# Both seven-product phases of a transformer layer in a written order of all engines, with other chunks in the first down projection

## The chip, the cores and the metric

The kernel runs on one core of a Trainium2 chip. A core has TensorE (PE, matmuls into eight PSUM banks), VectorE (DVE), ScalarE (ACT), GpSimd (POOL), SyncE (SP, which issues the transfers here) and 16 DMA engines. The metric is the time on the device of one execution, in microseconds (us), as the median of several runs. The profiled execution is a further one, and has its own time.

## The reference

One layer over 512 latent tokens and 256 context tokens, of width 1024, in float32. What matters here are its two feed-forward layers, FFN1 on all 768 tokens and FFN2 on the 512 latent ones:

```python
def swiglu(h, w1, w3, w2):
    return (jax.nn.silu(h @ w1) * (h @ w3)) @ w2

def ffn_sublayer(h_in, shift, scale, gate, norm_w, w1, w3, w2):
    h = modulate(rms_norm(h_in, norm_w), shift, scale)
    return h_in + 0.5 * gate * swiglu(h, w1, w3, w2)
...
    mx = jnp.split((jax.nn.silu(c) @ w_ada + b_ada)[:, None, :], N_MOD, axis=-1)
    x = ffn_sublayer(x, mx[0], mx[1], mx[2], norm1_w, ffn1_w1, ffn1_w3, ffn1_w2)
    ...
    x = ffn_sublayer(x, mx[6], mx[7], mx[8], norm3_w, ffn2_w1, ffn2_w3, ffn2_w2)
```

Between them lie attention and a gated MLP over chunks ("the middle" below). `w1` and `w3` are 1024 by 2816 each, `w2` is 2816 by 1024. The vectors `mx` and `mc` (shift, scale and gate) come from a product of `w_ada` (1024 by 9216) with one vector for each kind of token.

## The kernel before

**Numbers.** A float32 operand is split into a rounded high part and a remainder: a cast on ACT (L103) and a subtraction on VectorE (L104), both into buffers of `Stream` with five slots (`OPS`). `mm3` (L128) multiplies with three matmuls: high by high (L131), high by low (L132), low by high (L133).

**Up projection.** The 2816 columns are 22 tiles of 128, numbered f. For f = 0 and 1 they are computed while the modulation vectors arrive, for f = 2 and 3 plainly (`up1`), and from f = 4 on by `Winograd` (L593): one f with both weights is a 2 by 2 block problem, solved with seven products instead of eight. Each product (`prod`, L588) is four k-tiles of `mm3`, so 12 matmuls, of 384 columns in FFN1 and 256 in FFN2. The tokens' sums (B11, T1 and so on) are made once ahead of the phase. The weights' sums are made for each unit f from a 1 MB block (two `block` buffers): an addition (L607) and three subtractions (L629 to L631), on GpSimd; for FFN2's first unit they are on VectorE. So a unit needs seven operands of 128 by 512, each split by ACT and VectorE.

A unit has four accumulators X, Y, Z, W. In `head` it is product B11 into X, copied to p1. In `mid` T1 goes into Z, B21 into X (then silu into sl), T2 into Y (then u2 = Y + p1, L636) and T3 into W (then u3 = W + u2 and u3 = Z + u3, L638 and L639). In `tail` T4 is added into W (then times sl, and split into the tile g: L649, L650 and `g_split`, L325) and B22 into Z (then silu, times u3, and split). For even f the accumulators are four single banks `mm`; for odd f they are two tiles `big` of two banks each, with X and Z in one and Y and W in the other. `run` (L660) traces `head` of f + 1 between `mid` and `tail` of f.

**Down projection.** After some units a chunk of n tiles g is multiplied with its rows of `w2` (`down`): for each of eight output tiles and each column group (two of 384 in FFN1, one of 512 in FFN2) one `mm` bank gets 3n matmuls and is added into x by VectorE (L340 in FFN1, with an instruction of 256 columns for the latent and one of 128 for the context tokens of a group; L346 in FFN2). Its weights come in 512 KB pieces into three `raw` buffers. FFN1's chunks are 3, 3, 4, 4, 3, 5 and FFN2's 4, 4, 4, 4, 2, 4. FFN1's last chunk runs with the normalisation of the middle.

**The modulation vectors.** From f = 2 on, 80 dots (L234, one `w_ada` piece of 128 by 1024 with the vector, on VectorE, its piece in a `raw` buffer) are traced in small steps: eight behind f = 2 and f = 3 each, then four to a unit.

**What sets the order.** A tile scheduler orders the instructions of each engine by its own estimate of time, starting from the traced program; only what is traced through `Pinned` (L49) or `keep_in_program_order` keeps the written order. Before, both seven-product phases and their downs are left to the scheduler. The start, and the stretch ahead of FFN2's units (with `nc.ordered` set), are pinned on VectorE, ACT and GpSimd.

Of the kernel before, what the change touches and what calls it, by code (L numbers as in the profile page):

```python
# [8 lines left out]
F32 = mybir.dt.float32  # L9
# [7 lines left out]
P = 128  # L17
D = 1024
NK = D // P
# [7 lines left out]
SCALE = QH ** -0.5  # L27
CHUNKS1 = [3, 3, 4, 4, 3, 5]
CHUNKS2 = [4, 4, 4, 4, 2, 4]
# [30 lines left out]
class Core:  # L60


    def __init__(self, tc):
        self.nc, self.ordered = tc.nc, False
        self.pinned = {e: Pinned(tc, getattr(tc.nc, e)) for e in ("vector", "scalar", "gpsimd")}

    def __getattr__(self, name):
        return self.pinned[name] if self.ordered and name in self.pinned else getattr(self.nc, name)


class Halves:
# [65 lines left out]
def layer_kernel(ctx: ExitStack, tc: tile.TileContext, xT, wfirst, wst, wada, wuq, wkpe, cols, wrope, vnw, rope, out):  # L137
# [8 lines left out]
    ps = ctx.enter_context(tc.tile_pool(name="ps", bufs=1, space=PSUM))  # L146

    def big():
        return ps.tile([P, 2, 512], F32, tag="big", bufs=2, name=f"big_{nc.next_id()}")
# [374 lines left out]
    def g_tile(f):  # L524
        pool, bufs = (gp, 3) if f % 5 < 3 else (gp2, 2)
        gt[f] = tuple(pool.tile([P, 768], F32R, tag=t, bufs=bufs, name=f"{t}_{nc.next_id()}") for t in ("gh", "gl"))
        return gt[f]
# [28 lines left out]
    def down(f0, n, u0, groups, evac, dts=range(NK), cache=None):  # L556
        us = {} if cache is None else cache
        for dt in dts:
            for g, gn in groups:
# [9 lines left out]
                evac(pt, dt, g, gn)  # L569

    starts1 = [sum(CHUNKS1[:i]) for i in range(len(CHUNKS1))]
    starts2 = [sum(CHUNKS2[:i]) for i in range(len(CHUNKS2))]
# [19 lines left out]
    class Winograd:  # L592
# [16 lines left out]

        def head(self, f):  # L610
            n = self.n
            if self.ready[0] != f:
                self.prep(f)
            q, s1, eng = self.ready[1:]
            a11 = st.operand(q[0])
            bigs4 = bigs(4) if f % 2 else None
            mms = None if f % 2 else [mm() for _ in range(4)]
            banks = [bigs4[i] for i in (0, 2, 1, 3)] if f % 2 else [mms[i] for i in (0, 1, 3, 2)]
            prod(banks[0], a11, self.blocks["B11"], n)
            p1 = self.tmp("p1", n)  # L620
            nc.scalar.copy(p1, banks[0][:, :n])  # L621
            return q, s1, banks, p1, eng

        def mid(self, hd):
            n, bl = self.n, self.blocks
            q, s1, (X, Y, Z, W), p1, eng = hd
            prod(Z, st.operand(s1), bl["T1"], n)
            prod(X, st.operand(q[1]), bl["B21"], n, False)
            eng.tensor_sub(q[2], q[0], q[2])  # L629
            eng.tensor_sub(q[0], s1, q[0])  # L630
            eng.tensor_sub(q[1], q[1], q[0])  # L631
            sl = self.tmp("sl", n, self.sl_bufs)
            nc.scalar.activation(sl, X[:, :n], AF.Silu)
            prod(Y, st.operand(q[0]), bl["T2"], n)
            u2, u3 = self.tmp("u2", n), self.tmp("u3", n)
            nc.vector.tensor_add(u2, Y[:, :n], p1)  # L636
            prod(W, st.operand(q[2]), bl["T3"], n)
            nc.vector.tensor_add(u3, W[:, :n], u2)  # L638
            nc.vector.tensor_add(u3, Z[:, :n], u3)  # L639
            return u2, u3, sl  # L640

        def tail(self, f, hd, md):
            n, bl = self.n, self.blocks
            q, s1, banks, p1 = hd[:4]
            X, Y, Z, W = (b[:, :n] for b in banks)
            u2, cB, sl = md
            gh, gl = self.g_tile(f)
            prod(W, st.operand(q[3]), bl["T4"], n, False)
            nc.vector.tensor_add(W, W, u2)  # L649
            nc.vector.tensor_mul(W, W, sl)  # L650
            g_split(W, gh[:, :n], gl[:, :n])
            prod(Z, st.operand(q[1]), bl["B22"], n, False)
            nc.vector.tensor_add(Z, Z, u2)
            nc.scalar.activation(Z, Z, AF.Silu)
            nc.vector.tensor_mul(Z, Z, cB)
            g_split(Z, gh[:, n:], gl[:, n:])

        def run(self, f0, after, step=lambda i: None):
            hd = self.head(f0)
            for f in range(f0, NF):  # L660
                md = self.mid(hd)
                step(0)
                nxt = self.head(f + 1) if f + 1 < NF else None
                step(1)
                self.tail(f, hd, md)
                step(2)
                hd = nxt
                after(f)

# [10 lines left out]

    def after1(f):
        if f < NPLAIN1:
            ada_step(8)
        for ci, n in enumerate(CHUNKS1[:-1]):
            if f == (5 if ci == 0 else (starts1[ci] + n + 1) // 2 * 2):
                down(starts1[ci], n, U_DN1 + starts1[ci], [GA, GB], lambda pt, dt, g, gn: evac_x(pt, dt, seg_of(g // 384), 0))

    t1ctx = ExitStack()
    for f in range(NFIRST, NPLAIN1):
        up1(f, U_UP1, gp, (hh, hl), [GA, GB])  # L690
        if f == NFIRST:
# [6 lines left out]
            B12 = blocks["T1"]  # L698
            half = lambda k0, g0, i: hf[:, k0 + i, g0 : g0 + 384]
            wt = lambda tag, n, b: gp.tile([P, n], F32, tag=tag, bufs=b, name=f"tt_{nc.next_id()}")[:, :384]  # L700
            tmps = [wt("p1", 384, 1), wt("u2", 384, 1), wt("u3", 384, 1), wt("s1", 512, 2)]
            for i in range(4):
                b11, b12, b21, b22 = (half(k0, g0, i) for k0 in (0, 4) for g0 in (0, 384))
# [8 lines left out]
            gp2 = fctx.enter_context(tc.tile_pool(name="ffn1h", bufs=2))  # L712
        after1(f)
# [641 lines left out]

    def after2(f):
        for ci, n in enumerate(CHUNKS2[:-1]):
            if f == starts2[ci] + n:
                down(starts2[ci], n, U_DN2 + starts2[ci], [(0, 512)], lambda pt, dt, g, gn: evac_lat(pt, dt, 2))

    wino.run(NPLAIN2, after2)
    lastu = {}
# [4 lines left out]
    hbctx.close()  # L1367
    hactx.close()


# [97 lines left out]
```

## Time and profile before

| | us |
|---|---|
| median of three runs (1194.44 to 1204.01) | 1196.52 |
| profiled execution, its own time | 1193.31 |
| span of the profile | 1191.5 |
| PE busy | 1148.8 |
| DVE busy | 928.8 |
| ACT busy | 539.9 |
| POOL busy | 372.2 |

The mean granted clock of TensorE in that execution is 0.994 of full speed. In the timeline FFN1's seven-product units begin at about 116 us and end at about 545 us, its last down projection and the normalisation reach to about 612 us. FFN2's units begin at about 884 us and their last product is at about 1150 us. Where rows of the profile are shown, a name such as L104 is a line of the kernel before; `opl<-block,oph` is output and inputs. A busy TensorE may still run slowly, since matmuls are pipelined and a matmul's shown duration is longer than the step from one to the next. "Idle before" is the time an engine waited, with the instruction that released it.

### The profile page before, as it was taken

What the parts mean: (1) busy time and instruction counts of PE and PEld (TensorE: products, weight loads), DVE (VectorE), ACT (ScalarE), POOL (GpSimd) and SP (SyncE); (2) the same over time, 40 slices, a digit from 0 to 9 for tenths busy, and PEclk for the clock granted to TensorE, in tenths of its full rate; (3) what the DMA queues carried; (4) which work ended last, traced back from release to release, by engine and by line L of the source; (5) the groups of instructions that cost most, each with busy time, mean ns of one, the idle gap of its engine ahead of it and who ended that gap; (6) DMA issues with size and microseconds to landing.
All of it is one profiled execution on the core that took longest, in us unless ns stands there. A gap on an engine that the chain in (4) does not pass through costs nothing. (4 is left out here: it accounts for less than half of the span.)

```text
span 1191.5 us, 18866 instructions
## 1 busy us (share of the span) xinstructions
PE 1148.8 (96%) x7070; PEld 1070.5 (90%) x7070; DVE 928.8 (78%) x1686; ACT 539.9 (45%) x1093; POOL 372.2 (31%) x329
## 2 busy tenths in 40 slices
PE   9999899999999999999999999999999999999998
PEld 5689899989999989999878879898898989899997
DVE  4799987898987977667963978776976868787784
ACT  5563322233243233244653538996553535354451
POOL 0001411341142042124334845883101524243330
PEclk9999999999999999999999999999999999999999
DMA  9434333233643733224221311102112332223212
GB/s 353 143 142 160 109 122 101 90 115 121 208 162 103 241 116 124 86 90 137 94 85 60 118 36 36 37 1 71 36 40 103 107 107 107 106 76 137 107 36 89
DMA packets 35371, 128.52 MB, mean 108 GB/s; under 512 B 3664, under 2 KB 10576, under 8 KB 29776
## 3 DMA queue, kind: packets, MB, share of 16 engines
q1 hardware_dynamic: 35136, 127.25, 31.4%
q8 instruction: 56, 0.92, 0.3%
q14 instruction: 35, 0.29, 0.1%
q10 hardware_dynamic: 144, 0.06, 0.0%
HBM read 125.20 MB, written 2.10 MB: 107 GB/s over the span
## 5 line engine op out<-in xcount | busy, mean ns | idle before, releaser
L103 ACT CAST oph<-block 128x512 fp32r<-128x512 f32 x216 | 133.9, 622 | 245.1 <-PE mm L132 167.9
L104 DVE TENSOR_TENSOR opl<-block,oph 128x512 fp32r<-128x512 f32 x216 | 190.5, 885 | 35.0 <-ACT oph L103 33.0
L131 PE MATMUL mm<-gh,oph 128*128 128x384 f32 (+2 forms) x532 | 186.7, 353 | 4.0 <-DVE x L340 2.2
L132 PE MATMUL mm<-gl,oph 128*128 128x384 f32 (+2 forms) x532 | 187.0, 351 | 0.0
L133 PE MATMUL mm<-gh,opl 128*128 128x384 f32 (+2 forms) x532 | 185.4, 352 | 1.4 <-DVE opl L104 1.4
L103 ACT CAST oph<-raw 128x512 fp32r<-128x512 f32 x140 | 85.7, 619 | 118.1 <-PE mm L132 68.0
L607 POOL TENSOR_TENSOR s<-block 128x512 f32<-128x512 f32 x35 | 54.1, 1546 | 238.4 <-DVE g L259 111.0
L631 POOL TENSOR_TENSOR block<-block 128x512 f32<-128x512 f32 x35 | 47.9, 1367 | 239.6 <-DVE opl L104 239.6
L104 DVE TENSOR_TENSOR opl<-raw,oph 128x512 fp32r<-128x512 f32 x140 | 106.4, 766 | 19.8 <-ACT oph L103 19.3
L131 PEld LDWEIGHTS mm<-gh,oph 128*128 128x128 f32 x532 | 99.9, 188 | 11.5 <-ACT oph L103 2.1
L133 PEld LDWEIGHTS mm<-gh,opl 128*128 128x128 f32 x532 | 99.8, 188 | 8.4 <-DVE opl L104 1.9
L132 PEld LDWEIGHTS mm<-gl,oph 128*128 128x128 f32 x532 | 99.9, 188 | 6.6
L630 POOL TENSOR_TENSOR block<-s,block 128x512 f32<-128x512 f32 x35 | 52.8, 1509 | 168.9 <-DVE opl L104 168.1
L340 DVE SCALAR_TENSOR_TENSOR x<-mm,g,x 128x256 f32<-128x256 f32 x194 | 70.9, 409 | 18.2 <-PE mm L133 18.2
L131 PE MATMUL big<-hh,oph 128*128 128x384 f32 (+1 forms) x240 | 80.1, 334 | 3.4 <-ACT p L621 1.7
L346 DVE SCALAR_TENSOR_TENSOR x<-mm,g,x 128x512 f32<-128x512 f32 x55 | 41.0, 749 | 50.4 <-PE mm L133 50.4
L132 PE MATMUL big<-hl,oph 128*128 128x384 f32 (+1 forms) x240 | 79.8, 333 | 0.0
L133 PE MATMUL big<-hh,opl 128*128 128x384 f32 (+1 forms) x240 | 79.4, 331 | 0.0
L234 DVE SCALAR_TENSOR_TENSOR junk<-raw,cb 128x1024 bf16<-128x1024 f32 x48 | 66.7, 1391 | 3.9 <-DMA raw<-wada 3.5
L131 PE MATMUL mm<-hh,oph 128*128 128x384 f32 x160 | 54.9, 343 | 3.4 <-ACT oph L103 2.3
L629 POOL TENSOR_TENSOR block<-block 128x512 f32<-128x512 f32 x35 | 56.2, 1607 | 2.7
L132 PE MATMUL mm<-hl,oph 128*128 128x384 f32 x160 | 54.8, 343 | 2.2 <-DVE hl L323 2.2
(584 smaller groups left out, 3351.5 us busy)
## 6 DMA issues: line engine op xcount, KB each, us to landing
raw<-wst SPq DMA_DIRECT2D x82, 512.0 KB, 3.7
block<-wst SPq DMA_DIRECT2D x36, 1024.0 KB, 4.9
raw<-wada SPq DMA_DIRECT2D x56, 512.0 KB, 4.1
block<-wada SPq DMA_DIRECT2D x7, 1024.0 KB, 7.7
x<-xT SPq DMA_DIRECT2D x6, 512.0 KB, 6.5
raw<-wfirst SPq DMA_DIRECT2D x8, 256.0 KB, 6.0
out<-x SPq DMA_DIRECT2D x7, 256.0 KB, 2.2
block_first<-wada SPq DMA_DIRECT2D x2, 512.0 KB, 8.0
```

What stands on the lines that cost most here:

```text
L103: self.pin(self.nc.scalar.copy(dst[0], src))
L104: self.pin((eng or self.nc.vector).tensor_sub(dst[1], src, dst[0].bitcast(F32)))
L131: nc.tensor.matmul(out, lh, rh, start=first, stop=False, skip_group_check=more)
L132: nc.tensor.matmul(out, lh, rl, start=False, stop=False, skip_group_check=more)
L133: nc.tensor.matmul(out, ll, rh, start=False, stop=last, skip_group_check=more)
L234: nc.vector.scalar_tensor_tensor(out, raw, 1.0, cb[:, which, :], ALU.mult, ALU.mult, accum_out=acc[which][:, c : c + 1] if to is None else to,
L340: nc.vector.scalar_tensor_tensor(x[:, dt, s0 : s0 + sn], pt[:, o : o + sn], mod_g[i][which][:, dt : dt + 1], x[:, dt, s0 : s0 + sn], ALU.m ...
L346: nc.vector.scalar_tensor_tensor(lat(x, dt), two(pt), mod_g[i][0][:, dt : dt + 1], lat(x, dt), ALU.mult, ALU.add)
L607: (eng or nc.gpsimd).tensor_add(s1, q[2], q[3])
L629: eng.tensor_sub(q[2], q[0], q[2])
L630: eng.tensor_sub(q[0], s1, q[0])
L631: eng.tensor_sub(q[1], q[1], q[0])
```

## The change

- `Core.ordered` can be "all", which pins TensorE too. It is set around both seven-product phases, their downs included. SyncE's queue is not pinned.
- A class `Flow` writes the order. It has a list of operand splits that are still to do and holds at most five (`OPS`) alive. Each product or output tile of a down is a slot: first the first part of the evacuation of the product before, then the splits that have become possible (those for four slots ahead), then a filler (a dot), then the rest of that evacuation; and then the product's matmuls.
- The products of a unit stand in a fixed order: T1, B21, T2, T3 of f, then B11 of f + 1, then T4 and B22 of f.
- In odd units the accumulators are four single banks `one` instead of two tiles of two banks. The pool of those banks is closed and opened again around each phase.
- FFN1's chunks are 5, 5, 6, 6 and their downs follow units 6, 10 and 16; the last is again in the middle. The tiles g of FFN1 have seven buffers in place of five. FFN2's chunks stay.
- The dots: four behind f = 2 and f = 3 each; three to a unit up to f = 6, two to a unit after that; in a down one or two to an output tile (chunks of five) or two (the chunk of six).

```diff
-CHUNKS1 = [3, 3, 4, 4, 3, 5]
+CHUNKS1 = [5, 5, 6, 6]
+DOWN1 = [6, 10, 16]
...
-        self.pinned = {e: Pinned(tc, getattr(tc.nc, e)) for e in ("vector", "scalar", "gpsimd")}
+        self.pinned = {e: Pinned(tc, getattr(tc.nc, e)) for e in ("vector", "scalar", "gpsimd", "tensor")}
...
+class Flow:
+    def __init__(self, size):
+        self.size, self.live, self.spent = size, 0, 0
+        self.todo, self.ready, self.pend = deque(), deque(), []
+
+    def fill(self):
+        while self.todo and self.live < self.size:
+            self.ready.append(self.todo.popleft()())
+            self.live += 1
+
+    def take(self):
+        if not self.ready:
+            self.fill()
+        return self.ready.popleft()
+
+    def slot(self, filler=lambda: None):
+        pend, self.pend = self.pend, []
+        for g in pend:
+            next(g, None)
+        self.live -= self.spent
+        self.spent = 0
+        self.fill()
+        filler()
+        for g in pend:
+            for _ in g:
+                pass
...
+    def one():
+        return half[0].tile([P, 512], F32, tag="one", bufs=4, name=f"one_{nc.next_id()}")
...
+    def down_flow(flow, f0, n, groups, evac, step=lambda dt: None):
+        pairs, gone = [], 0
+        for dt in range(NK):
+            flow.slot(lambda: step(dt))
+            while 4 * len(pairs) < dt * n + n:
+                pairs.append(flow.take())
...
+            for (g, gn), pt in zip(groups[:-1], pts):
+                evac(pt, dt, g, gn)
+            def last(pt=pts[-1], dt=dt, g=groups[-1]):
+                evac(pt, dt, *g)
+                yield
+            flow.pend = [last()]
...
+        def product(self, bank, blk, first, pend, step=None):
+            flow = self.flow
+            a = flow.take()
+            flow.slot(step or (lambda: None))
+            prod(bank, a, self.blocks[blk], self.n, first)
+            flow.spent = 1
+            flow.pend = [pend] if pend else []
...
+            banks = [one() if f % 2 else mm() for _ in range(4)]
...
+            def ev_u3():
+                v.tensor_add(u3, W, u2)
+                v.tensor_add(u3, Z, u3)
+                yield
+            def ev_lo():
+                v.tensor_add(W, W, u2)
+                v.tensor_mul(W, W, sl)
+                yield
+                g_split(W, gh[:, :n], gl[:, :n])
...
+            self.product(banks[2], "T1", True, None)
+            self.product(banks[0], "B21", False, ev_sl(), lambda: step(f, 0))
+            self.product(banks[1], "T2", True, ev_u2(), lambda: step(f, 1))
+            self.product(banks[3], "T3", True, ev_u3())
+            nxt = None
+            if f + 1 < NF:
+                nxt = self.open(f + 1, None)
+            self.product(banks[3], "T4", False, ev_lo(), lambda: step(f, 2))
+            self.product(banks[2], "B22", False, ev_hi())
...
-        if f < NPLAIN1:
-            ada_step(8)
...
+    def after1(flow, f):
+        for ci in ends1(f):
+            down_flow(flow, starts1[ci], CHUNKS1[ci], [GA, GB], lambda pt, dt, g, gn: evac_x(pt, dt, seg_of(g // 384), 0),
+                      lambda dt: ada_step(2 if CHUNKS1[ci] > 5 else 1 + dt % 2))
+
+    def ada_up(f, i):
+        if f <= DOWN1[0] or i < 2:
+            ada_step()
...
+        ada_step(4)
...
-    Winograd(gp, 384, U_UP1, blocks, g_tile, 1).run(NPLAIN1, after1, lambda i: ada_step(1 + (i == 1)))
+    nc.ordered = "all"
+    Winograd(gp, 384, U_UP1, blocks, g_tile, 1).run(
+        NPLAIN1, lambda f: [(CHUNKS1[ci], U_DN1 + starts1[ci]) for ci in ends1(f)], after1, ada_up)
+    ada_step(99)
+    nc.ordered = False
...
-    wino.run(NPLAIN2, after2)
+    nc.ordered = "all"
+    wino.run(NPLAIN2, lambda f: [(CHUNKS2[ci], U_DN2 + starts2[ci]) for ci in ends2(f)], after2)
+    nc.ordered = False
```

More of the change, by code (lines that the diff above doesn't have):

```diff
@@ L1 @@
+from collections import deque
 from contextlib import ExitStack
@@ L146, in layer_kernel, with other_banks @@
     ps = ctx.enter_context(tc.tile_pool(name="ps", bufs=1, space=PSUM))
+    half_ctx = ExitStack()
+    half = []
+    def other_banks():
+        half_ctx.close()
+        half[:] = [half_ctx.enter_context(tc.tile_pool(name=f"ps{nc.next_id()}", bufs=1, space=PSUM))]
+    other_banks()
     def big():
-        return ps.tile([P, 2, 512], F32, tag="big", bufs=2, name=f"big_{nc.next_id()}")
+        return half[0].tile([P, 2, 512], F32, tag="big", bufs=2, name=f"big_{nc.next_id()}")
+    def one():
+        return half[0].tile([P, 512], F32, tag="one", bufs=4, name=f"one_{nc.next_id()}")
     def mm():
@@ L658, in run, with wants, first, third @@
-        def run(self, f0, after, step=lambda i: None):
-            hd = self.head(f0)
-            for f in range(f0, NF):
[L661 to L668, printed above, removed]
+        def wants(self, f):
+            q, s1, eng = [], [], []
+            def first():
+                if self.ready[0] != f:
+                    self.prep(f)
+                q[:], s1[:], eng[:] = self.ready[1], [self.ready[2]], [self.ready[3]]
+                a = st.operand(q[0])
+                eng[0].tensor_sub(q[2], q[0], q[2])
+                eng[0].tensor_sub(q[0], s1[0], q[0])
+                return a
+            def third():
+                a = st.operand(q[1])
+                eng[0].tensor_sub(q[1], q[1], q[0])
+                return a
+            of = lambda i: lambda: st.operand(q[i])
+            return first, lambda: st.operand(s1[0]), third, of(0), of(2), of(3), of(1)
@@ L670, in evac_part, with run @@
+        def run(self, f0, downs, after, step=lambda f, i: None):
+            other_banks()
+            self.plan(f0, downs)
+            hd = self.open(f0, None)
+            for f in range(f0, NF):
+                hd = self.unit(f, hd, step)
+                after(self.flow, f)
+            self.flow.slot()
+            other_banks()
     def evac_part(pt, dt, g, n):
@@ L702, in layer_kernel @@
             for i in range(4):
-                b11, b12, b21, b22 = (half(k0, g0, i) for k0 in (0, 4) for g0 in (0, 384))
+                b11, b12, b21, b22 = (part(k0, g0, i) for k0 in (0, 4) for g0 in (0, 384))
                 nc.vector.tensor_sub(tmps[i], b12, b11)
```

121 lines of the change are left out of this document (67 added, 54 removed).

## The prediction

> **What bounds the kernel now.** I read the table of busy time by engine first, then busy time by stretch, then TensorE's waits inside the stretches that change, and the timeline at the longest of them.
>
> ```profile
> PE 1148.8 (96%) x7070; PEld 1070.5 (90%) x7070; DVE 928.8 (78%) x1686; ACT 539.9 (45%) x1093; POOL 372.2 (31%) x329
> ```
>
> TensorE is the bound, and the change leaves its matrix products as they are: it can win only time in which TensorE stands or runs slowly. By stretch (start and end, length, then busy time and instruction count of PE, PEld, DVE, ACT, POOL, then granted clock, DMA share and GB/s):
>
> ```profile
> 116.00:148.00 32.00, 26.21 (x136) 24.60 (x135) 32.00 (x43) 10.51 (x21) 13.81 (x9) 0.95 0.29 97
> 148.00:240.00 92.00, 92.00 (x531) 92.00 (x532) 74.17 (x149) 24.54 (x45) 19.46 (x12) 1.00 0.31 105
> 240.00:260.00 20.00, 17.36 (x96) 16.39 (x95) 20.00 (x32) 8.84 (x19) 7.29 (x4) 0.99 0.33 106
> 260.00:420.00 160.00, 156.70 (x890) 155.36 (x889) 137.28 (x251) 47.78 (x88) 36.98 (x24) 0.99 0.49 167
> 420.00:545.00 125.00, 122.47 (x703) 121.89 (x704) 84.90 (x155) 43.08 (x81) 31.43 (x27) 1.00 0.29 101
> 545.00:560.00 15.00, 12.68 (x72) 12.07 (x71) 12.79 (x23) 8.73 (x17) 6.23 (x10) 1.00 0.38 122
> 560.00:612.00 52.00, 48.74 (x281) 43.81 (x280) 45.42 (x84) 31.02 (x62) 25.49 (x21) 1.00 0.26 83
> 884.00:893.00 9.00, 9.00 (x79) 9.00 (x78) 7.86 (x14) 4.69 (x10) 1.83 (x1) 1.00 0.01 3
> 893.00:1150.00 257.00, 254.77 (x1759) 236.36 (x1758) 197.85 (x325) 114.23 (x225) 91.04 (x63) 1.00 0.30 103
> ```
>
> The seven-product stretch of FFN1 lies in the first five rows. From 148 to 240 us TensorE has no gap: 531 matmuls in 92.00 us are 0.173 us each, so a product of 12 matmuls is 2.08 us and a unit of seven 14.55 us. In 116–148 TensorE is idle 5.79 us, and VectorE is busy all 32.00 us; in 240–260 it is idle 2.64 us with VectorE busy all 20.00. There VectorE is the bound. The other two rows have 3.30 and 2.53 us. Sum 14.3 us. The waits of TensorE from 116 to 545 us (total, times, longest) have the same sum:
>
> ```profile
> PE big L131 <- DVE u L636: 4.2, 2, 2.8
> PE mm L131 <- ACT oph L103: 4.1, 2, 2.3
> PE big L131 <- ACT p L621: 1.7, 1, 1.7
> PE mm L133 <- DVE opl L104: 1.7, 2, 1.2
> PE mm L131 <- DVE x L340: 1.3, 2, 0.8
> PE mm L131 <- DVE u L638: 0.6, 2, 0.4
> PE big L131 <- ACT oph L103: 0.6, 1, 0.6
> ```
>
> Twelve stops. The first is the shared tile: a `big` tile is two banks, and in odd units Y and W are its two halves, so T3's matmul into W waits until VectorE has read Y (L636), though it doesn't need Y. The timeline shows the longest (start, duration):
>
> ```profile
> 417.97 0.33 PE L131 MATMUL mm<-hh,oph 128*128 128x384 f32 x1
> 418.14 0.34 PE L132 MATMUL mm<-hl,oph 128*128 128x384 f32 x1
> 421.26 0.44 PE L131 MATMUL big<-u3h,oph 128*128 128x384 f32 x1 [2.78 <-DVE u L636]
> ```
>
> Matmuls start 0.17 us apart, then 3.12 us pass, 2.95 more than the step; the row says 2.78 idle. So a stop costs about 0.17 us more than its idle time: twelve stops, 2.0 us. Two stops are also followed by slow matmuls; this is the second:
>
> ```profile
> 260.02 0.52 PE L132 MATMUL mm<-hl,oph 128*128 128x384 f32 x1
> ...
> 262.88 0.34 PE L133 MATMUL big<-u3h,opl 128*128 128x384 f32 x1
> ```
>
> Nine steps of 0.32 us, 2.86 us instead of 9 x 0.173 = 1.56: 1.3 us lost. The granted clock of 0.95 in 116–148 is the first such place (0.05 x 32 = 1.6 us). **FFN1's loss is 14.3 + 2.0 + 2.9 = 19.2 us.** Its end (545–560 and 560–612, the normalisation in the second) has 2.32 and 3.26 us idle. FFN2 has 2.23 us from 893 to 1150, and nothing at its start (884–893).
>
> **The change, part by part.** Durations (busy time, mean ns) first, FFN1 148–545 us, then FFN2 893–1150 us:
>
> ```profile
> L104 DVE TENSOR_TENSOR opl<-block,oph 128x512 fp32r<-128x512 f32 x95 | 80.1, 846 | 19.9 <-ACT oph L103 19.0 <-PE mm L133 0.9
> L340 DVE SCALAR_TENSOR_TENSOR x<-mm,g,x 128x256 f32<-128x256 f32 x80 | 38.2, 478 | 15.4 <-PE mm L133 15.4
> L234 DVE SCALAR_TENSOR_TENSOR junk<-raw,cb 128x1024 bf16<-128x1024 f32 x24 | 33.7, 1404 | 3.4 <-DMA raw<-wada 3.2
> L340 DVE SCALAR_TENSOR_TENSOR x<-mm,g,x 128x128 f32<-128x128 f32 x80 | 27.2, 340 | 0.0
> L638 DVE TENSOR_TENSOR u<-big,u 128x384 f32<-128x384 f32 x9 | 5.0, 556 | 8.9 <-PE big L133 8.8
> ```
>
> ```profile
> L104 DVE TENSOR_TENSOR opl<-block,oph 128x512 fp32r<-128x512 f32 x94 | 87.1, 927 | 14.9 <-ACT oph L103 14.1
> L638 DVE TENSOR_TENSOR u<-big,u 128x256 f32<-128x256 f32 x8 | 3.4, 425 | 2.5 <-PE big L133 2.5
> ```
>
> *Chunks.* FFN1's down projection goes from six chunks to four. A chunk is evacuated by 16 instructions of 256 columns and 16 of 128 columns (8 rows, two groups, two segments), so 64 go: 32 x 0.478 + 32 x 0.340 = 26.2 us of VectorE. That isn't TensorE time where VectorE has slack; it is in 240–260.
>
> *Ada dots.* The 16 dots traced at f = 2 and 3 become 8; the rest moves into the units (3, later 2 a unit) and the downs. From 92 to 148 us VectorE is full, and 8 x 1.40 = 11 us leave it before the first unit. This, with splits prepared four slots ahead, takes most of the 116–148 loss: 5.79 idle, 4 stops x 0.17, 1.6 slow, about 8 us. What is late next: the first unit's own splits, T1's and then the first operand's, two ACT casts and VectorE subtractions behind each other. I take 1.3 us left (bounds 0 and 3).
>
> *Four single banks.* The two L636 waits in FFN1 (4.2 us) lose their cause. What is late next is u3's read of W. T4 adds into W only after u3's first addition (L638). The scheduler often put two or three products between T3 and T4; the written order has one, B11 of the next unit: 2.08 us of cover in FFN1, 1.40 in FFN2 (two thirds of the columns). VectorE must not lag by more than cover less addition: 2.08 - 0.56 = 1.5 us, and 1.40 - 0.43 = 1.0 us.
>
> *Does it lag?* A unit on VectorE: seven splits, nine two-input operations, in FFN1 two or three dots. FFN1: 7 x 0.846 + 9 x 0.556 + 2 x 1.40 = 13.7 us against 14.55, with three dots 15.1. Only the units at f = 4 to 6 have three: lag 0.55 a unit, so I take 0.5 us of stall at two of them. A down slot of five has 1 to 2 dots and about one split: at most 2 x (0.478 + 0.340) + 1.25 x 0.846 + 1.5 x 1.40 = 4.8 us, against 5 x 6 x 0.173 = 5.2; with six, 5.7 against 6.2. Both fit. FFN2: 7 x 0.927 + 9 x 0.425 = 10.3 us against 7 x 1.40 = 9.8: lag 0.5 a unit, 1.0 us of room, cleared in the next down. Of four units between downs the last two or three stall, about 0.3 us each, 10 of 18: **+3 us** (bounds 0 and 9, the whole 0.5 for each of 18).
>
> *Written order of all engines.* TensorE's matmul stream is now fixed; a late split stops everything behind it. The casts and subtractions of VectorE, ACT and POOL get fixed places, SyncE doesn't. At FFN2's start unit 4's splits now stand behind the last plain evacuation. Before, they ran at
>
> ```profile
> 884.03 0.69 DVE L104 TENSOR_TENSOR opl<-s,oph 128x512 fp32r<-128x512 f32 x1 [2.49 <-ACT oph L103]
> ```
>
> and so ahead of need. An operand's cast on ACT is
>
> ```profile
> L103 ACT CAST oph<-block 128x512 fp32r<-128x512 f32 x216 | 133.9, 622 | 245.1 <-PE mm L132 167.9
> ```
>
> After the last plain matmul now come that evacuation's four operations (silu, multiply, cast, subtraction; my estimate is 0.4 each, by the 425 ns of 256 columns), and behind them a cast of 0.6 and a subtraction of 0.69: 2.9 us, **+3 us** (bounds 0, if VectorE has caught up by then, and 4).
>
> *Transfers.* The landings (median) are
>
> ```profile
> raw<-wst SPq DMA_DIRECT2D x82, 512.0 KB, 3.7
> block<-wst SPq DMA_DIRECT2D x36, 1024.0 KB, 4.9
> ```
>
> A unit block's buffer comes free about half a unit of VectorE work ahead, 8.7 us in FFN1 and 6.5 in FFN2 by my count of the instructions, more than 4.9. In the long down of six rows, weights and dots share three raw buffers: 2.2 to 4.9 us of VectorE work stand between release and first use, against 3.7. VectorE will wait there; four `mm` banks cover some 5 us of TensorE. I take 1 us (bounds 0 and 3).
>
> *Sum.* FFN1: of 19.2 us stay 1.3 + 1.0 + 1.0 and 1.0 for small stops, 4.3: **-14.9**. End of FFN1: the last chunk has six rows instead of five, so 18 instead of 15 matmuls a bank run while normalisation starts, 8 x 2 x 3 x 0.173 = 8 us more TensorE work beside it; of its 3.26 us I take **-2** (bounds 0 and -3.3). FFN2: 2.23 idle goes to 6 less the three L636 stops it had, by the row
>
> ```profile
> PE big L131 <- DVE u L636: 6.2, 5, 2.8
> ```
>
> (5 stops in all, 2 of them in FFN1): 3 + 3 - 2.1 = **+3.9**. Sum -13.0: the profiled execution of 1193.31 us becomes 1180.3. The median of the runs shown is 3.2 us above that execution: **1183.5 us**.
>
> **A rule against it.** POOL's subtractions delay VectorE already: a 128x8 operation takes 0.16 us, and 1.25 beside a POOL operation.
>
> ```profile
> 413.52 0.16 DVE L254 TENSOR_TENSOR a<-accc,b 128x8 f32<-128x8 f32 x1
> ...
> 417.13 1.25 DVE L255 TENSOR_TENSOR a<-a,col 128x8 f32<-128x8 f32 x1
> 418.31 0.68 DVE L104 TENSOR_TENSOR opl<-block,oph 128x512 fp32r<-128x512 f32 x1
> ```
>
> ```profile
> 416.21 2.15 POOL L630 TENSOR_TENSOR block<-s,block 128x512 f32<-128x512 f32 x1 [12.53 <-DVE opl L104]
> ```
>
> The Trainium skill, page "SBUF — State Buffer", section "SBUF: two separate sides", says that VectorE's operations with two SBUF inputs and GpSimd's operations take a shared port pair in turn, for a whole instruction, and the other blocks. By that rule a unit's four POOL operations could hold VectorE for their whole length, which is rival 2's side. The trace agrees on the mechanism: the 1.25 us end with the POOL operation, at 418.4.
>
> A split's subtraction is 0.68 us free, 0.846 and 0.927 on the mean: POOL costs VectorE 7 x 0.17 = 1.2 us a unit in FFN1 and 7 x 0.25 = 1.7 in FFN2. The scheduler could put a PSUM operation first; a written order can't.
>
> **The rivals.**
> 1. *One product of cover isn't enough.* VectorE is late at u3 in most units: 0.5 us in each of 36 (18 in each FFN) is 18 us in place of my 4: 1197.5, and half of it 1188.5. For it: FFN2's 10.3 against 9.8. Against it: 148–240 us ran at 74.17 of 92 without a stop.
> 2. *Slower: POOL's hold doubles in the fixed order*, so a split's subtraction in FFN2 is 0.68 + 2 x 0.25 = 1.18 us: a unit is 7 x 1.18 + 3.8 = 12.1 us of VectorE against 9.8, TensorE waits 2.3 us for each of 18 units, less 1.0 of room at each of five groups: +36, in place of my 3. With 13 gained elsewhere: 1216; it is slower than before from a mean of about 1.02 us on (0.9 us a unit, 16 us), and by over 1% from 1.12. For it: four POOL operations a unit, of up to the 2.15 us above. Against it: half of the hold is chance overlap now, and the scheduler's order was not made to avoid it.
> 3. *The change takes only the start*: the loss of 116–148 goes (6.7 us), the later stops only change their name as VectorE is as full as before, and FFN2 gives back 3: 1193. The L636 stop at 421 speaks for it: a dot stood before u2's read.
> 4. *Better*: FFN2 adds nothing, since before it did the same work with 2.23 us idle: 1177.
>
> The Trainium skill, page "TensorE: Matmul & The Clock Gate", section "Why this matters for your kernels", says that only an idle time of over about 3 us drops the clock. The trace differs: the slow steps from 260.02 follow a stop of 2.33 us, and after the 2.78 us at 421.26 the next matmuls aren't slow (the row of 260–420 grants 0.99). By the rule my new stops of 1.3 and 2.9 us cost nothing more; by the trace each may cost 1.3 more, 1186 at worst.
>
> **How the numbers follow.** Forecast (1179 to 1189) 0.50; rival 4 (1173 to 1179) 0.15; rivals 1 and 3 (1189 to 1198) 0.23; rival 2 (over 1205) 0.12. One per cent, about what a measurement of this kernel can tell from no change, is 1184.6 and 1208.5. Faster by more: 0.15 and 0.36 of the forecast's 0.50, 0.51. Slower by more: 0.11. Within: 0.38. The range 1174 to 1198 leaves out rival 2 and a twentieth below.
>
> **What would show it.** In the profile after: fewer than 6 us of TensorE idle from 110 to 545; no wait on L636's counterpart; 64 fewer evacuations (the group of 256 columns, 80 from 148 to 545 us, loses 32); waits of TensorE on u3's addition mostly in FFN2; a stop of about 3 us where unit 4 begins; a mean subtraction below 1.0 us there. The forecast is wrong if that mean rises over 1.0, if TensorE waits for operand casts unit after unit, or if raw transfers in the six-row downs land over 5 us.

## The result and the profile after

The changed kernel takes 1181.88 us (median of 6 runs, 1181.65 to 1182.74) against 1197.51 us (6 runs, 1194.44 to 1204.01): a ratio of 0.9865, 95% interval 0.9839 to 0.9891. It is faster, by 1.1 to 1.6%. Its profiled execution took 1182.46 us, that of before 1193.31.

The table of busy time by engine, of the changed kernel:

```profile
PE 1145.3 (97%) x7070; PEld 1072.2 (91%) x7070; DVE 901.2 (76%) x1624; ACT 540.6 (46%) x1095; POOL 361.1 (31%) x329
```

VectorE has 62 instructions and 28 us less. Where TensorE's time went shows busy time by stretch (start and end, length, then PE, PEld, DVE, ACT, POOL, granted clock, DMA share, GB/s), here of after:

```profile
75.00:110.00 35.00, 30.24 (x166) 29.52 (x167) 26.78 (x51) 12.23 (x27) 2.59 (x2) 0.95 0.34 105
110.00:150.00 40.00, 37.75 (x216) 37.14 (x215) 32.78 (x48) 17.35 (x34) 15.72 (x10) 1.00 0.20 65
150.00:549.00 399.00, 397.97 (x2295) 397.46 (x2295) 319.98 (x574) 137.95 (x253) 99.11 (x80) 1.00 0.43 144
549.00:594.00 45.00, 43.13 (x248) 40.02 (x247) 39.86 (x70) 26.85 (x54) 19.39 (x16) 0.96 0.21 65
865.00:880.00 15.00, 13.17 (x97) 12.77 (x96) 8.90 (x15) 6.48 (x14) 1.65 (x1) 0.89 0.05 7
880.00:1145.00 265.00, 259.99 (x1797) 241.03 (x1796) 202.25 (x336) 114.92 (x231) 89.75 (x64) 1.00 0.29 100
```

FFN1's written order runs 399 us with 1.03 us of TensorE idle. The first units, from 110 to 150 us, have 2.25 us idle. But from 75 to 110 us, ahead of the written order, TensorE is idle 4.76 us, where it was 2.10 in the kernel before:

```profile
75.00:110.00 35.00, 32.90 (x192) 32.18 (x193) 34.20 (x64) 13.10 (x28) 0.00 (x0) 1.00 0.41 134
```

And FFN2, from 880 us on, is idle 5.01 us where before it was 2.23. TensorE's waits in FFN2 after (total, times, longest):

```profile
PE mm L59 <- DVE u L59: 1.9, 4, 0.7
PE mm L59 <- ACT p L59: 1.7, 4, 0.5
PE mm L59 <- ACT oph L59: 1.6, 1, 1.6
PE one L59 <- DVE u L59: 0.9, 2, 0.6
PE one L59 <- ACT p L59: 0.5, 1, 0.5
PE mm L59 <- DVE opl L59: 0.2, 1, 0.2
```

All pinned instructions have the line of the pinning helper, L59, so one goes by tile names. The waits for `oph` and `opl` are the start of unit 4, 1.8 us together. The others are all T4 behind B11 of the next unit, eleven times, as here (timeline, start and duration):

```profile
933.02 0.27 PE L59 MATMUL mm<-b11h,opl 128*128 128x256 f32 x1
933.25 0.41 DVE L59 TENSOR_TENSOR u<-one,u 128x256 f32<-128x256 f32 x1
933.81 0.36 PE L59 MATMUL one<-t4h,oph 128*128 128x256 f32 x1 [0.51 <-ACT p L59]
```

T4 adds into W, so it needs VectorE's first addition for u3 (the DVE line), which reads W. Five of the eleven waits are put down to ACT's copy into p instead, which T4 doesn't touch; but in all eleven T4 starts 0.14 to 0.15 us after the first addition ends (here 933.66), and at 1060.22 the copy is not even done. So all eleven wait for VectorE.

For the comparison of kernels I worked one number out of each timeline: the loss, the sum over TensorE's matmuls of the step to the next one less the clean step (0.173, 0.117 and 0.227 us for 384, 256 and 512 columns). Steps within 0.03 us of the clean one are left out. So it holds stops and slow matmuls. The stretches are cut at marks of the program: "FFN1 on" goes from 150 us to the first matmul of the middle's normalisation, "norm." is the 45 us behind it, FFN2 its units and last down.

| loss, us | 75–110 | 110–150 | FFN1 on | norm. | FFN2 |
|---|---|---|---|---|---|
| before | 2.7 | 8.7 | 15.2 | 4.8 | 4.7 |
| after | 6.8 | 2.8 | 1.4 | 3.8 | 11.5 |
| ffn1_only | 7.8 | 2.8 | 0.3 | 3.4 | 4.8 |
| ffn2_only | 2.8 | 10.4 | 20.9 | 4.8 | 11.5 |
| banks_only | 2.7 | 7.3 | 13.5 | 4.8 | 0.9 |
| chunks_only | 2.7 | 10.6 | 22.1 | 3.5 | 5.9 |
| all_but_order | 6.6 | 0.0 | 26.5 | 3.5 | 0.2 |
| flow_big | 6.3 | 6.7 | 14.5 | 3.5 | 19.5 |
| t1_early | 5.0 | 2.7 | 0.7 | 3.5 | 14.9 |
| b21_late | 6.6 | 2.7 | 0.3 | 3.5 | 16.5 |
| hoist3 | 6.6 | 2.8 | 0.8 | 3.4 | 7.8 |
| dots_8 | 3.5 | 5.7 | 0.1 | 3.5 | 10.4 |
| ffn2_free_84 | 3.7 | 2.8 | 0.3 | 3.5 | 1.3 |
| no_pool2 | 6.5 | 2.5 | 0.3 | 3.5 | 4.0 |

In the two profiled executions FFN1 wins 5.9 + 13.8 + 1.0 = 20.7 us, 75–110 loses 4.1, FFN2 loses 6.8. That is 9.8 of the 10.85 us between them. Each row is one execution, and where the scheduler orders, executions of the same order differ: up to 867 us TensorE, VectorE, ACT and GpSimd do the same instructions in the same order in ffn2_only as in before, and yet ffn2_only loses 10.4 + 20.9 us in FFN1 where before loses 8.7 + 15.2. So differences of some 7 us between FFN1 rows of the scheduler's order may be such scatter.

### The profile page after: what moved, and what is told of

Same layout as the page of the kernel before. It is cut to its first block, busy times and chain, and to the rows that moved or that the text cites. A ratio compares the mean times of both kernels' runs of the same rounds, so it can differ in the third digit from the quotient of the medians.

```text
span 1180.7 us, 18802 instructions
## 1 busy us (share of the span) xinstructions
PE 1145.3 (97%) x7070; PEld 1072.2 (91%) x7070; DVE 901.2 (76%) x1624; ACT 540.6 (46%) x1095; POOL 361.1 (31%) x329
## 5 line engine op out<-in xcount | busy, mean ns | idle before, releaser
L59 POOL TENSOR_TENSOR block<-block 128x512 f32<-128x512 f32 x70 | 106.3, 1518 | 378.4 <-DVE opl L59 375.7
L59 DVE TENSOR_TENSOR opl<-block,oph 128x512 fp32r<-128x512 f32 x216 | 188.0, 879 | 34.6 <-ACT oph L59 32.6
L59 ACT CAST oph<-block 128x512 fp32r<-128x512 f32 x216 | 134.0, 621 | 148.6 <-PE mm L59 96.6
L59 PE MATMUL mm<-gh,oph 128*128 128x384 f32 (+1 forms) x400 | 141.6, 354 | 0.0
L59 PE MATMUL mm<-gl,oph 128*128 128x384 f32 (+1 forms) x400 | 141.6, 354 | 0.0
L59 PE MATMUL mm<-gh,opl 128*128 128x384 f32 (+1 forms) x400 | 141.6, 354 | 0.0
L59 DVE SCALAR_TENSOR_TENSOR x<-mm,g,x 128x256 f32<-128x256 f32 (+2 forms) x152 | 71.5, 507 | 59.1 <-PE mm L59 53.5
L59 POOL TENSOR_TENSOR s<-block 128x512 f32<-128x512 f32 x35 | 50.1, 1432 | 152.1 <-DVE junk L281 100.1
L59 ACT CAST oph<-raw 128x512 fp32r<-128x512 f32 x84 | 51.2, 620 | 90.2 <-PE mm L59 63.8
L59 POOL TENSOR_TENSOR block<-s,block 128x512 f32<-128x512 f32 x35 | 46.3, 1323 | 115.3 <-DVE opl L59 114.7
L59 PEld LDWEIGHTS mm<-gh,opl 128*128 128x128 f32 x400 | 75.1, 188 | 5.7
L59 PEld LDWEIGHTS mm<-gh,oph 128*128 128x128 f32 x400 | 75.1, 188 | 5.5
L59 PEld LDWEIGHTS mm<-gl,oph 128*128 128x128 f32 x400 | 75.1, 188 | 5.4
L59 DVE TENSOR_TENSOR opl<-raw,oph 128x512 fp32r<-128x512 f32 x84 | 56.3, 684 | 6.4 <-ACT oph L59 6.3
L59 DVE SCALAR_TENSOR_TENSOR junk<-raw,cb 128x1024 bf16<-128x1024 f32 x40 | 50.8, 1275 | 1.7 <-DMA raw<-wada 1.5
L59 PE MATMUL one<-hh,opl 128*128 128x384 f32 x144 | 48.4, 336 | 0.0
L59 PE MATMUL one<-hl,oph 128*128 128x384 f32 x144 | 48.4, 336 | 0.0
L59 PE MATMUL one<-hh,oph 128*128 128x384 f32 x144 | 48.4, 336 | 0.0
L59 PE MATMUL mm<-hh,oph 128*128 128x384 f32 x144 | 48.4, 336 | 0.0
L59 PE MATMUL mm<-hl,oph 128*128 128x384 f32 x144 | 48.4, 336 | 0.0
```

The source lines that it names most:

```text
L59: return lambda *a, **k: self.tc.keep_in_program_order(f(*a, **k))
```

## The experiments

The kernels of one group ran beside the same runs of before (medians 1199.14, 1199.77, 1201.40 and 1200.47 us), so ratios are compared across groups.

**Which phase gains: one phase alone.**

```diff
 # ffn1_only: FFN2 as in the kernel before
-    wino = Winograd(f2, 256, ...)
-    nc.ordered = "all"
-    wino.run(NPLAIN2, lambda f: [...], after2)
+    wino = Free(f2, 256, ...)      # head, mid, tail and run of before
+    wino.run(NPLAIN2, after2)      # with down of before
```

> The changed kernel with FFN2's units and downs traced as before and left to the scheduler; FFN1 as changed. Theory A (the gain is all FFN1's, and FFN2's written order costs about 5 us through the stops of T4 behind u3 and at unit 4): about 1177 us, the eleven T4 stops and the stop of 1.6 us at unit 4 gone, the three stops of 0.7 us of T3 behind u2 back. Rival B (FFN2's written order is worth something too): 1184 or more.

Measured: 1176.18 us, ratio 0.9803 (0.9770 to 0.9835). Theory A's 1177 holds: FFN2's loss goes from 11.5 to 4.8, and its three stops of T3 behind u2 are back.

```profile
PE big L166 <- DVE u L829: 2.1, 3, 0.7
```

```diff
 # ffn2_only: FFN1 (chunks, dots, banks, order) as in the kernel before
-CHUNKS1 = [5, 5, 6, 6]
+CHUNKS1 = [3, 3, 4, 4, 3, 5]
-    nc.ordered = "all"
-    Winograd(gp, 384, ...).run(NPLAIN1, lambda f: [...], after1, ada_up)
+    Free(gp, 384, ...).run(NPLAIN1, after1, lambda i: ada_step(1 + (i == 1)))
```

> The kernel before with only FFN2's units and downs in the written order (four single banks there); FFN1 with its old chunks, dots and order. Theory A: slower than before by about 5 us, 1202 us, TensorE idle in FFN2 7 us instead of 2.2. Rival B: 1194 or less.

Measured: 1208.65 us, ratio 1.0064 (1.0040 to 1.0089): slower. Its FFN2 has the 11.5 us of loss of the changed kernel. So FFN2's written order costs: 0.6% by this run, and by ffn1_only 0.9865 - 0.9803, also 0.6%. All the gain is FFN1's. Against FFN2 in the scheduler's order with single banks (banks_only and ffn2_free_84 below) the written order loses still more: 11.5 us against 0.9 and 1.3.

**What of FFN1's change gains: banks, chunks, or all but the order.**

```diff
 # banks_only: kernel before, in head()
-            bigs4 = bigs(4) if f % 2 else None
-            mms = None if f % 2 else [mm() for _ in range(4)]
+            banks = [one() if f % 2 else mm() for _ in range(4)]
 # chunks_only: kernel before
-CHUNKS1 = [3, 3, 4, 4, 3, 5]
+CHUNKS1 = [5, 5, 6, 6]
+DOWN1 = [6, 10, 16]
 # all_but_order: kernel before with both of these, and
-            ada_step(8)
+            ada_step(4)
```

> The kernel before with four single banks in odd units of both phases, order left to the scheduler. Theory A: the waits of T3 on u2 (6.2 us of idle) go, but half comes back as waits of T4 on u3 or of splits, since VectorE is as full: 1194 us. Rival C (the false dependency on the shared tile was most of what the order won): 1188 us or less.

> The kernel before with FFN1's chunks 5, 5, 6, 6, downs after units 6, 10 and 16 and seven buffers of g; order, banks and dots as before. Theory A: the stops of 240 to 262 us (4.6 us with the slow matmuls) and those at 546 and 551 us (2.7 us) go, the start from 116 to 148 us stays: 1190 us. Rival D (64 evacuations less, 26 us of VectorE, is the whole gain and the order nothing): 1182 us. Rival E (chunks alone do nothing): 1196 us.

> The kernel before with everything of the change but the written order: four single banks in both phases, chunks 5, 5, 6, 6 with their downs and seven buffers of g, four dots behind f = 2 and f = 3 and four to a unit. The scheduler orders. Theory A (banks and order need each other in FFN1; the scheduler leaves VectorE's backlog at 116 and around the downs): 1188 us, as the banks alone (1187.3). Rival I (order is worth nothing once banks, chunks and dots are there): 1180 us or less.

Measured: banks_only 1187.28 us, 0.9892 (0.9853 to 0.9930); chunks_only 1200.15 us, 1.0012 (0.9994 to 1.0030); all_but_order 1195.73 us, 0.9960 (0.9942 to 0.9977). The banks alone give 1.1%, more than theory A said and just rival C's 1188; by the intervals they can't be told from the whole change (0.9839 to 0.9891). Their waits in FFN2 are all gone (loss 0.9). In FFN1 others stand in their place (110 to 565 us):

```profile
PE mm L168 <- DVE opl L139: 6.0, 4, 3.0
PE mm L166 <- DVE x L387: 4.1, 4, 1.8
PE one L168 <- DVE opl L139: 2.2, 2, 1.8
```

The chunks alone give nothing: rival E holds, my theory's 1190 falls. The 64 evacuations, 26 us, are gone, but VectorE's whole busy time falls by 14 us only (928.8 to 914.6). In the scheduler's order a stop of 7.7 us comes, in which a unit's first product waits for a `big` tile, the start stays, and so does the stop that before has at 259.5 us (2.30 us, at 255.2):

```profile
PE big L166 <- DVE gl L374: 8.1, 2, 7.7
PE mm L166 <- ACT oph L138: 4.9, 3, 2.3
```

Everything but the order gives 0.4%; theory A's 1188 is missed too, by 8 us. The start from 110 to 150 is free of loss (0.0; with eight dots banks_only and chunks_only have 7.3 and 10.6). But the units' operand splits come late in the scheduler's order: the two longest stops, 4.93 us at 355.5 and 4.74 us at 477.1, are products of units that wait for a split, and VectorE works on dots ahead of it (five between 343.4 and 354.1 us). From 110 to 572 us TensorE waits

```profile
PE mm L168 <- DVE opl L139: 10.9, 4, 4.9
PE one L168 <- DVE opl L139: 3.8, 3, 1.5
PE one L166 <- ACT p L813: 2.7, 1, 2.7
```

and its loss is 26.5 us. Rival I falls: with the chunks and dots there, FFN1's order is worth 25 us of loss (26.5 to 1.4). The places of the dots in the units and downs belong to that order; they were not tried apart from it. Without the order chunks and dots take away what the banks gave (0.9960 against 0.9892).

**Is the order worth anything without the banks?**

```diff
 # flow_big: changed kernel, in open()
-            banks = [one() if f % 2 else mm() for _ in range(4)]
-            banks = [banks[i] for i in (0, 1, 3, 2)]
+            bigs4 = bigs(4) if f % 2 else None
+            mms = None if f % 2 else [mm() for _ in range(4)]
+            banks = [bigs4[i] for i in (0, 2, 1, 3)] if f % 2 else [mms[i] for i in (0, 1, 3, 2)]
```

> The changed kernel with two tiles of two banks for the accumulators of odd units, as before, in place of four single banks. In the written order T3 follows T2, so in each odd unit T3 into W must wait until VectorE has read Y: by the addition and its release about 0.8 us each in 18 units, and slow matmuls behind some: theory A 1197 us. Rival H (the banks matter little, TensorE makes up for it elsewhere): 1185 us.

Measured: 1208.92 us, 1.0080 (1.0054 to 1.0107), worse than theory A's 1197. In 16 units T3 waits for the read of u2, 1.5 us on the mean where I had 0.8:

```profile
PE big L59 <- DVE u L59: 23.9, 16, 2.4
```

The order needs the banks: without them the changed kernel is slower than before. The banks don't need the order.

**The stop at 92 us: the dots.** In the timeline of after:

```profile
92.30 0.34 PE L168 MATMUL big<-hh,opl 128*128 128x384 f32 x1
95.91 0.45 PE L166 MATMUL big<-hh,oph 128*128 128x384 f32 x1 [3.27 <-DVE sl L381]
...
97.27 0.53 PE L167 MATMUL big<-hl,oph 128*128 128x384 f32 x1
97.59 0.53 PE L168 MATMUL big<-hh,opl 128*128 128x384 f32 x1
```

The stop comes 72 matmuls after f = 2's first, so ahead of its fourth accumulation. `up1` puts that into the second bank of a `big` tile, and f = 2's evacuation (`sl`, at 95.3 us) is still reading the first bank of that tile: a shared tile once more. With four dots behind f = 2 the scheduler, which still orders this stretch, put three splits of f = 3 (85.6, 88.6 and 92.8 us) ahead of that evacuation on VectorE. Ten slow matmuls follow.

```diff
 # dots_8: changed kernel
-        ada_step(4)
+        ada_step(8)
```

> The changed kernel with eight dots behind f = 2 and f = 3 each, as before, instead of four (and so fewer at the end). Theory A (the new stop of 3.3 us at 92 us and the slow matmuls behind it come from the scheduler's order of the f = 3 splits ahead of f = 2's evacuation, which four dots made): the loss from 75 to 110 us goes from 6.8 back to 2.7, and VectorE, idle for 10 us before 115, has room for eight dots, so 110 to 150 stays near 3 to 4: 1178.5 us. Rival G (the dots were what made 116 to 148 lose 8.7): that loss comes back, 1184 us.

Measured: 1180.32 us, 0.9845 (0.9824 to 0.9866): 0.2% against the changed kernel, within the intervals. The loss of 75–110 goes from 6.8 to 3.5 as theory A said, but half of rival G is true as well: 110–150 goes from 2.8 to 5.7, with a stop that is again followed by slow matmuls:

```profile
118.34 0.60 PE L59 MATMUL mm<-hh,opl 128*128 128x384 f32 x1 [1.82 <-DVE opl L59]
118.74 0.53 PE L59 MATMUL mm<-hh,oph 128*128 128x384 f32 x1
119.06 0.53 PE L59 MATMUL mm<-hl,oph 128*128 128x384 f32 x1
```

So eight behind f = 2 and four behind f = 3 was tried, together with FFN2 left to the scheduler, now with single banks:

```diff
 # ffn2_free_84: as ffn1_only, with banks_only's accumulators in FFN2, and
-        ada_step(4)
+        ada_step(8 if f == NFIRST else 4)
```

> FFN1 in the written order; FFN2 left to the scheduler as before, but with four single banks; and eight dots behind f = 2, four behind f = 3. Theory A: against the run with FFN2 left as before (1176.2) the three T3 stops go (2.4 us) and, with the order of 80 to 101 us as before, the stop at 92 falls from 3.3 to 0.8 us without its slow matmuls (4 us), while unit 4 starts as in the changed kernel: 1170 us. Rival G: the dots cost the start of unit 4 what they save, 1174 us.

Measured: **1169.64 us, 0.9728 (0.9701 to 0.9754)**, the fastest kernel here, and theory A's 1170. 75–110 has 3.7, 110–150 still 2.8, FFN2 1.3.

**FFN2's T4 stops: cover, or VectorE?** Two kernels give T4 two products of cover:

```diff
 # t1_early: order of FFN2's products
-T1, B21, T2, T3 of f, B11 of f + 1, T4, B22
+B21, T2, T3 of f, B11, T1 of f + 1, T4, B22
 # b21_late
+T1, T2, T3, B21 of f, B11 of f + 1, T4, B22
```

> The changed kernel with another product order in FFN2 alone: T1 of the next unit is moved ahead too, so B11 and T1 of f + 1 stand between T3 and T4 of f (2.8 us of cover instead of 1.4). Theory A (the eleven T4 stops, some 6.8 us from start to start, come from VectorE's lag against one product of cover): they go, 1176 us. Rival F (VectorE's work per unit is over TensorE's, so the wait only moves to another product or split): 1180 us or more.

> The changed kernel with another product order in FFN2 alone: T1, T2, T3, B21, then B11 of f + 1, T4, B22. So two products, 2.8 us, stand between T3 and T4, and T1, whose end needs no evacuation, stays behind B22, whose evacuation goes to and fro between VectorE and ACT. Theory J (T4 stops because VectorE, 88% busy and the rest of the time waiting for ACT in the fixed order, is up to 2 us behind at u3): they go, 6 us, 1176 us. Rival F (the lag grows until it fills whatever cover there is, as with T1 moved): 1181 us or more.

Measured: t1_early 1185.60 us, 0.9883 (0.9860 to 0.9907); b21_late 1189.14 us, 0.9895 (0.9872 to 0.9917). By their medians both are slower than the changed kernel, and rival F holds. The stops didn't go. In t1_early six are left, but of some 1.6 us of idle each instead of 0.5; b21_late has eleven, six of them of 1.2 us. A stretch of about one unit, from one T4 to the next, says why (first of after, then of b21_late, of t1_early and of ffn2_free_84):

```profile
922.70:933.10 10.40, 10.00 (x86) 9.87 (x84) 9.23 (x17) 5.61 (x12) 5.83 (x4) 1.00 0.31 102
```

```profile
932.96:944.21 11.25, 10.04 (x86) 9.87 (x84) 9.75 (x17) 5.56 (x13) 5.47 (x4) 1.00 0.26 93
```

```profile
931.15:942.80 11.65, 10.03 (x86) 9.87 (x84) 9.67 (x17) 5.49 (x13) 6.14 (x4) 1.00 0.26 91
```

```profile
917.50:927.70 10.20, 10.09 (x86) 9.87 (x84) 10.05 (x17) 5.71 (x13) 6.16 (x4) 1.00 0.29 104
```

TensorE needs 9.8 us for the 84 matmuls of a unit. In the scheduler's order (last row) VectorE works 10.05 of 10.20 us and just keeps up: TensorE has no wait at all from 860 to 1150 us there. In the written order VectorE works less but waits for ACT, in after for operand casts and for g's cast (waits of VectorE, 922.7 to 943.8 us):

```profile
DVE gl L59 <- ACT gh L59: 0.9, 2, 0.4
DVE opl L59 <- ACT oph L59: 0.9, 2, 0.5
```

So in the written order a unit ends when VectorE has gone round, its work and its waits, and more cover between T3 and T4 does not shorten that round. Why the two other product orders make it longer, by some 0.8 and 1.2 us, stays open.

What fills VectorE? The operand subtractions in those units of after and of the scheduler's order (busy time, mean ns):

```profile
L59 DVE TENSOR_TENSOR opl<-block,oph 128x512 fp32r<-128x512 f32 x12 | 11.1, 951 | 1.0 <-ACT oph L59 0.9
```

```profile
L139 DVE TENSOR_TENSOR opl<-block,oph 128x512 fp32r<-128x512 f32 x12 | 13.2, 1118 | 0.1
```

```diff
 # no_pool2: changed kernel; GpSimd's four operations of FFN2's units left out from f = 5 on
-            (eng or nc.gpsimd).tensor_add(s1, q[2], q[3])
+            if self.n == 256 and eng is None:
+                self.ready = f, q, q[3], None
+                return
...
-                eng[0].tensor_sub(q[2], q[0], q[2])
+                if eng[0]:
+                    eng[0].tensor_sub(q[2], q[0], q[2])
```

> The changed kernel without GpSimd's addition and three subtractions of FFN2's units from f = 5 on (the operands are split from the block as it came, so the second layer's result is not the reference's); all splits, products and the order of the other engines stay. Theory K (the T4 stops are VectorE's lag, and the lag is GpSimd's hold on the operand subtractions): their mean falls from 951 ns to about 680 within the units, a unit needs 1.6 us less of VectorE, and the eleven T4 stops go: 6.8 us, 1175 us. Rival L (the order's waits between VectorE and ACT alone are enough): the stops stay at 0.5 us, 1180 us.

Measured: 1172.24 us, 0.9765 (0.9744 to 0.9786). All eleven T4 stops are gone; what is left in FFN2 is the start of unit 4 (860 to 1140 us):

```profile
PE mm L59 <- ACT oph L59: 1.6, 1, 1.6
PE mm L59 <- DVE opl L59: 0.2, 1, 0.2
```

and the subtraction takes (876 to 1140 us, then after over 876 to 1150):

```profile
L59 DVE TENSOR_TENSOR opl<-block,oph 128x512 fp32r<-128x512 f32 x118 | 81.0, 686 | 22.8 <-ACT oph L59 21.3
```

```profile
L59 DVE TENSOR_TENSOR opl<-block,oph 128x512 fp32r<-128x512 f32 x104 | 94.6, 920 | 14.4 <-ACT oph L59 12.8
```

Theory K holds: without GpSimd's operations beside it VectorE isn't late. The waits for ACT are still there (21.3 us), and alone they cost TensorE nothing. Leaving the operations out also frees the splits from waiting for their results. But in after no wait of VectorE or ACT from 880 to 1145 us names GpSimd, and the subtractions themselves got shorter, by 6 x 0.265 = 1.6 us a unit against stops of 0.6. The hold alone stops nothing either: in ffn2_free_84 a subtraction takes 1118 ns, in the scheduler's order, and TensorE doesn't wait. The stops need both, the longer subtractions and the written order.

**The start of unit 4 in FFN2.**

```diff
 # hoist3: changed kernel
+    wino.plan(NPLAIN2, lambda f: [...])
+    wino.flow.size = 3
+    wino.flow.fill()
+    wino.flow.size = OPS
     evac(3, 1)
```

> The changed kernel with unit 4's first three splits of FFN2 (and the block's subtractions between them) traced ahead of the last plain evacuation. Theory A: the stop of 2.1 us where FFN2's units begin goes, 1180 us. Rival: the evacuation is late instead and the stop moves into unit 4, 1182 us.

Measured: 1178.14 us, 0.9821 (0.9798 to 0.9844). The stop is gone, and 3.7 us of loss with it (11.5 to 7.8), more than the 1.8 us of idle, since the slow matmuls behind it (the clock of 0.89 in 865–880: 0.11 x 15 = 1.65 us) go too.

## Why the prediction was right, and where it was wrong

The forecast was 1183.5 us with faster by over 1% as likeliest; it is 1181.88 and 1.35%. The mechanism was right: the gain is in FFN1, the loss in FFN2. That the total is so close is in part luck, since larger differences of the terms cancel.

- **FFN1, -14.9 and -2 at its end: right in kind, too small, and the 4.3 us that were to stay fit by luck.** 3.28 us of idle stay from 110 to 549 us, 4.2 measured as loss, but not where the sum had them (waits of TensorE, 110 to 549 us):

```profile
PE mm L59 <- ACT oph L59: 2.6, 2, 1.5
PE big L166 <- DVE sl L381: 0.7, 1, 0.7
```

The first row is T4 of two units (133.8 and 164.2 us) waiting for ACT's cast, 2.6 us where I had 1.0 of VectorE's lag; the second is f = 3, ahead of the written order. The first splits of unit 4 (1.3) and the transfers (1.0) cost TensorE nothing; VectorE waited 7.7 us for the dots' pieces, and in the six-row down the landings took 4.1 and 4.7 us. With the end the gain is 20.7 us instead of 16.9. The end's term was mis-sized: the stops at 546 and 551 us went as well, 2.7 us which I had left in, and the normalisation gave 1.0 instead of 2.

- **"Four single banks": the price of the shared tile was too low.** I credited the L636 waits. Banks_only shows 1.1% by themselves, and flow_big 23.9 us of waits where the order is written without them.
- **"Chunks: isn't TensorE time where VectorE has slack": right**, and the gain I gave them in 240–260 isn't theirs: chunks_only is 1.0012 and keeps that stop.
- **The dots: the first half right, the second missed.** VectorE's load from 110 to 150 fell as worked out and the loss with it, 8.7 to 2.8. That fewer dots would change the scheduler's order ahead of it was not in the sum: +4.1 us.
- **"A stop of about 3 us where unit 4 begins": right in kind; the size fits by luck.** It is 1.8 us of idle, not 2.9; with the restart and the slow matmuls, which the sum left out, it is some 3.7, and hoist3 removes 3.7.
- **"Does it lag?" (+3 in FFN2): right in kind, too small, and one step false.** Eleven stops where I had ten, and the last three of four units between downs, as I had it; but 0.6 us each with the restart instead of 0.3: 6.8 us. The false step is that the room between T3 and T4 decides how much stalls: with two products of room the loss grew (11.5 to 14.9 and 16.5). VectorE's round is the bound. With 10.3 us a unit I had its sum right by means that were not those of the units: it is 9.2 of work in the unit shown and about 0.9 of waiting for ACT (1.8 in two units).
- **Rival 2, POOL's hold: not in the form I gave it.** The mean over FFN2 went from 927 to 920 ns, so the fixed order doesn't double it, and "a written order can't" put another operation first was wrong as an argument: in the scheduler's order the hold is no shorter (1118 against 951 in the units shown). But without GpSimd's operations the T4 stops of the written order are gone, as no_pool2 shows.
- **The step from profile to median failed, and covered the rest.** The sum against the profiled execution was 1180.3, measured 1182.46. I added the 3.2 us by which before's median stood over its profile; the changed kernel's median is 0.6 us below its own. Before scatters over 9.6 us in six runs, after over 1.1. The granted clock goes with it: of the 44 executions of before beside the experiments the four fastest (1195.40 to 1196.19 us) had 0.993 to 0.996, the two slowest (1204.67 and 1204.98) 0.987. So before's profile, of 1193.31 us, is of one of its better executions. Most likely the 3.2 us belonged to before alone, where slow matmuls follow the same stop in one execution and not in another (last section), and the changed kernel has fewer such stops. What decides it stays open.

The Trainium skill, page "SBUF — State Buffer", section "SBUF: two separate sides", describes the mechanism of that hold, an exclusive lock between VectorE's operations with two SBUF inputs and GpSimd's. The runs agree: 686 ns without GpSimd's operations, 951 beside them.

## What to carry to other kernels

Here a written order paid where the engines had slack and was a loss where one was full. FFN1's stretch left VectorE a fifth (319.98 of 399 us busy) and ran 399 us almost without a stop; FFN2's units filled it with work and waits for ACT, and there the scheduler's order was better by 0.6%. Look for accumulators that share a tile before ordering anything: here that false dependency cost 1.1% by itself, nearly as much as the whole change won, and while it stood the written order was a loss. And when work is taken from a stretch that a scheduler orders, look at the stretch ahead of it too.

## What the runs showed of the hardware

- Slow matmuls (steps of 0.32 us instead of 0.173, for ten matmuls) followed stops of 1.82 us (118.3, dots_8), 2.33 (259.5, before) and 3.27 us (95.9, after), and in after the granted clock fell to 0.89 behind the stop of 1.6 us at unit 4. They did not follow the 2.78 us at 421 us of before. But in ffn2_only, which has the same order there, they follow the same stop:

```profile
427.38 0.45 PE L166 MATMUL big<-u3h,oph 128*128 128x384 f32 x1 [2.75 <-DVE u L829]
...
428.75 0.52 PE L166 MATMUL big<-u3h,oph 128*128 128x384 f32 x1
429.07 0.52 PE L167 MATMUL big<-u3l,oph 128*128 128x384 f32 x1
```

So the length of a stop alone doesn't decide it, it differs between executions of the same order, and a short stop can cost twice its idle time. The Trainium skill, page "TensorE: Matmul & The Clock Gate", section "Why this matters for your kernels", sets the limit at idle gaps of about 3 us; here shorter ones were enough.

- GpSimd's four operations a unit cost VectorE up to 0.44 us for each of six subtractions (1118 ns in two units of ffn2_free_84, against 674 for the seventh subtraction there and 686 in no_pool2; over all of FFN2 in after the mean is 920), and leaving them out of 17 units was worth 0.9765 against 0.9865, 1% of the whole kernel.
